# Attention scores: one DMA queue in place of two, and the last columns of the last tiles stored in three uneven pieces

## The chip, the core and the metric

The kernel runs on one core of one Trainium2 chip. A core has TensorE (PE), VectorE (DVE), ScalarE (ACT), GpSimd (POOL), SyncE (SP) and 16 DMA engines, which move data between the chip's main memory (HBM) and the core's working memory (SBUF). A DMA is issued by an engine's instruction queue (here SP's or ACT's) and its rows are dealt out over DMA engines. The metric is the device time of one execution in microseconds. Before the change it is 205.29 us, the median of three runs (205.13 to 205.38).

## The reference

```python
def setup_inputs():
    batch, heads, seq, dim = 8, 8, 512, 64
    # q, k: float32 of shape (8, 8, 512, 64)

def reference(q, k):
    scale = 1.0 / np.sqrt(q.shape[-1])
    return (np.einsum('bhqd,bhkd->bhqk', q, k) * scale).astype(np.float32)
```

For each of 64 pairs of batch and head, q times k transposed, scaled by 1/8. It reads 16.78 MB and writes 67.11 MB.

## The kernel before, in words

With B=8, H=8, S=512, D=64 the kernel's constants are P=128, G=4, M=32, R=16, RO=8, HP=2, U=64, JJ=2. It goes over the 8 batches.

- **Loads** (`load`, lines 53 to 58). For each batch one DMA for k (line 56) and one for q (line 57), each 1 MB: 128 partitions, in each two rows of 4 KB (heads 0 to 3 and 4 to 7). ACT's queue issues them. The raw tiles have four buffers, so four batches are loaded ahead (`AHEAD = 4`, lines 60 to 64); the load of batch b+4 stands in the code after the first two stores of batch b (lines 131 and 132).
- **Cast** (line 87): float32 to bfloat16, by DVE and ACT for the first batch, by POOL for all others.
- **Transposes**: PE transposes k (line 95) and q (line 103) into PSUM; DVE copies out kT (line 97), ACT qT (line 105).
- **Scores** (line 119): for each batch two groups `g0` (0 and 2) of two heads in each half `x`. A matmul gives 64 rows of 512 scores; eight of them fill two PSUM tiles.
- **Scaling** (`evacuate`, lines 68 to 75): ACT (line 71) and DVE (line 73) in turn multiply a PSUM tile by the scale and write it into an output tile.
- **Stores** (line 128): an output tile is 128 partitions of 8 x 512 float32, 16 KB per partition, 2 MB in all, contiguous in each partition and in HBM. There are two per group and four per batch, 32 in all, each stored by one DMA on SP's queue. The output tiles have six buffers: a buffer is written again when its store has landed.

The tile framework orders the instructions of each engine by its own planner, which may move an instruction ahead of its place in the code (the loads of the fifth batch go out before the first store). It also puts in the semaphores: DMA completions use eight of them in rotation, and the next DMA on a semaphore is issued only when the earlier one has landed.

Of the kernel before, what the change touches and what calls it, by code (L numbers as in the profile page):

```python
# [1 line left out]

# [5 lines left out]


@with_exitstack  # L10
def kernel(
    ctx: ExitStack,
    tc: tile.TileContext,
    q: bass.AP,
    k: bass.AP,
    out: bass.AP,
):

    nc = tc.nc
    B, H, S, D = q.shape
    scale = 1.0 / (D ** 0.5)
    P = 128
    G = H // 2
    M = P // G
    R = S // M
    RO = 8  # L30
    HP = RO * P // S
    U = P // HP
    JJ = R // RO

    f32 = mybir.dt.float32
    bf16 = mybir.dt.bfloat16

    q_r = q.rearrange("b (x g) (m j) d -> b (g m) x (j d)", x=2, j=R)
    k_r = k.rearrange("b (x g) (m j) d -> b (g m) x (j d)", x=2, j=R)
    out_r = out.rearrange("b (x n h) (u i) k -> b x n (h u) i k", x=2, h=HP, i=RO)  # L40

    consts = ctx.enter_context(tc.tile_pool(name="consts", bufs=1))
    raw_pool = ctx.enter_context(tc.tile_pool(name="raw", bufs=4))
    bf_pool = ctx.enter_context(tc.tile_pool(name="bf", bufs=2))
    t_pool = ctx.enter_context(tc.tile_pool(name="t", bufs=2))
    out_pool = ctx.enter_context(tc.tile_pool(name="out", bufs=6))
    tpsum_pool = ctx.enter_context(tc.tile_pool(name="tpsum", bufs=2, space=bass.MemoryType.PSUM))
    psum_pool = ctx.enter_context(tc.tile_pool(name="psum", bufs=3, space=bass.MemoryType.PSUM))

    AHEAD = 4  # L50
    raws = {}

    def load(b):
        kf = raw_pool.tile([P, 2, R * D], f32, name="kf")
        qf = raw_pool.tile([P, 2, R * D], f32, name="qf")
        nc.scalar.dma_start(out=kf, in_=k_r[b])  # L56
        nc.scalar.dma_start(out=qf, in_=q_r[b])  # L57
        raws[b] = (qf, kf)

    load(0)  # L60
    identity = consts.tile([P, P], dtype=bf16)
    make_identity(nc, identity)
    for b in range(1, AHEAD):
        load(b)

    n_evac = 0

    def evacuate(dst, src):
        nonlocal n_evac
        if n_evac % 2 == 0:  # L70
            nc.scalar.mul(out=dst, in_=src, mul=scale)  # L71
        else:
            nc.vector.tensor_scalar(out=dst, in0=src, scalar1=scale, scalar2=None,  # L73
                                    op0=mybir.AluOpType.mult)
        n_evac += 1

    for b in range(B):
        qf, kf = raws.pop(b)
        kb = bf_pool.tile([P, R, 2, D], bf16, name="kb")
        qb = bf_pool.tile([P, R, 2, D], bf16, name="qb")  # L80
        for slab, dst in ((kf, kb), (qf, qb)):
            for x in range(2):
                if b > 0:
                    copy = nc.gpsimd.tensor_copy
                else:
                    copy = (nc.vector.tensor_copy, nc.scalar.copy)[x]
                copy(out=dst[:, :, x, :], in_=slab[:, x].rearrange("p (j d) -> p j d", j=R))  # L87


        kT = t_pool.tile([P, P, R], bf16, name="kT")  # L90
        qT = t_pool.tile([P, RO, P, JJ], bf16, name="qT")
        for j0 in range(0, R, 8):
            tp = tpsum_pool.tile([P, 8, P], bf16, name="tp")
            for j in range(8):
                nc.tensor.transpose(out=tp[:, j, :], identity=identity,  # L95
                                    in_=kb[:, j0 + j].rearrange("p x d -> p (x d)"))
            nc.vector.tensor_copy(out=kT[:, :, j0:j0 + 8], in_=tp.rearrange("d j p -> d p j"))  # L97
        IW = 8 // JJ
        for i0 in range(0, RO, IW):
            tp = tpsum_pool.tile([P, IW, JJ, P], bf16, name="tp")  # L100
            for i in range(IW):
                for jj in range(JJ):
                    nc.tensor.transpose(out=tp[:, i, jj, :], identity=identity,  # L103
                                        in_=qb[:, RO * jj + i0 + i].rearrange("p x d -> p (x d)"))
            nc.scalar.copy(out=qT[:, i0:i0 + IW], in_=tp.rearrange("d i jj p -> d i p jj"))  # L105

        kTh = kT.rearrange("d (g m) j -> d g (m j)", g=G)
        qTh = qT.rearrange("d i (g m) jj -> d i g (m jj)", g=G)
        for g0 in range(0, G, 2):
            os = [out_pool.tile([P, 2 // HP, RO, S], f32, name="o") for _ in range(2)]  # L110
            for n in range(2 // HP):
                for i in range(0, RO, 2):
                    pss = [psum_pool.tile([P, 2, S], f32, name="ps") for _ in range(2)]
                    for w in range(2):
                        for h in range(HP):
                            g = g0 + n * HP + h
                            for x in range(2):
                                rows = slice(x * D, (x + 1) * D)
                                nc.tensor.matmul(out=pss[x][h * U:(h + 1) * U, w, :],  # L119
                                                 lhsT=qTh[rows, i + w, g, :],  # L120
                                                 rhs=kTh[rows, g, :],
                                                 start=True, stop=True,
                                                 tile_position=(x * D, h * U))
                    for x in range(2):
                        evacuate(os[x][:, n, i:i + 2, :], pss[x])
            for x in range(2):
                n0 = g0 // HP
                nc.sync.dma_start(  # L128
                    out=out_r[b, x, n0:n0 + 2 // HP].rearrange("n p i k -> p n (i k)"),
                    in_=os[x].rearrange("p n i k -> p n (i k)"))  # L130
            if g0 == 0 and b + AHEAD < B:
                load(b + AHEAD)


# [1 line left out]
_INS = ['q', 'k']  # L136
_OUTS = [((8, 8, 512, 512), 'float32')]


# [23 lines left out]
```

## Time and profile before

| | |
|---|---|
| median of 3 runs | 205.29 us |
| the profiled execution's own time | 205.29 us |
| its span, first to last instruction | 203.2 us |
| PE, DVE, ACT, POOL busy | 64%, 47%, 40%, 14% of the span |
| packets on the stores' queue and the loads' queue | 4608 and 4352 |
| mean DMA rate over the span | 413 GB/s |
| last store issued | 178.23 us |

The page gives, after the busy times, the span in 40 equal slices (5.08 us each): a digit is the busy share in tenths, and the row "DMA" is the mean over the core's 16 DMA engines. The queue lines give packets, megabytes and the share of the 16 engines' span that their packets took. A line of waits reads: engine and line, "<-" what it waited for, then us in total, how often, and the longest. The chain of waits follows the work that ended last back through what released it; its lines are start, duration and what it was. The view by stretches gives, for each, its length, the busy time and instruction count of PE, PE's weight loads, DVE, ACT and POOL, then PE's granted clock, the mean busy share of the DMA engines and GB/s; a transfer is counted where its packets start.

### The profile page before, as it was taken

The page shows a single profiled execution, that of the slowest core. Times are in us where ns is not written, and L with a number is a line of the kernel's source. Part 1 is how long each engine was busy: PE and PEld are TensorE (multiplying, and loading weights), DVE is VectorE, ACT ScalarE, POOL GpSimd, SP SyncE. Part 2 cuts the span into 40 slices and gives each one's busy share as a digit, 9 for nine tenths or more (in the row PEclk, how much of TensorE's full clock was granted, in tenths as well). Part 3 has the DMA queues.
Part 4 walks back from the last instruction along what each step waited for, and adds up shares of the span by engine and source line. Part 5 has one row for each costly group of instructions (what it writes and reads, how often), then busy time and mean ns, then how long its engine had stood idle before and what let it go on. Part 6 is the DMA issues. An engine that isn't in the chain of part 4 may idle for free.

```text
span 203.2 us, 1910 instructions
## 1 busy us (share of the span) xinstructions
PE 129.5 (64%) x768; PEld 46.5 (23%) x768; DVE 95.2 (47%) x82; ACT 81.9 (40%) x83; POOL 29.0 (14%) x34
## 2 busy tenths in 40 slices
PE   0187759997855099785997799779777777600000
PEld 0164314331520024210352135214211111000000
DVE  0247867567540291535853676276717180800000
ACT  0546753754852027242644273527551525200000
POOL 1077740303034003300030000000000000000000
PEclk9999985555785555555555555555555555555555
DMA  6999999999999999999999999999999999999991
GB/s 212 421 408 410 408 429 436 430 419 443 404 421 449 409 443 410 439 426 445 422 429 435 419 430 439 422 429 439 419 435 432 426 439 422 429 442 422 429 439 71
DMA packets 8968, 84.00 MB, mean 413 GB/s; under 512 B 768, under 2 KB 768, under 8 KB 4864
## 3 DMA queue, kind: packets, MB, share of 16 engines
q1 hardware_dynamic: 4608, 67.11, 77.3%
q10 hardware_dynamic: 4352, 16.78, 20.7%
q8 instruction: 6, 0.10, 0.2%
q14 instruction: 2, 0.02, 0.0%
HBM read 16.78 MB, written 67.11 MB: 413 GB/s over the span
## 4 chain that ended last, share of the span: by engine, by line
DMA 51%; DVE 17%; PE 14%; ACT 2%; POOL 1%; issue 1%; ACTq 1%; SPq 0%; DVEq 0%
DMA out_dram<-o 36%; DVE o L73 13%; DMA qf<-in_q_dram 11%; PE ps L119 10%; DVE kT L97 5%; DMA kf<-in_k_dram 4%; PE tp L95 2%; PE tp L103 2%; ACT o L71 2%; POOL kb L87 1%; ACT qT L105 1%; ACTq L56 0%; ACTq L57 0%; SPq L128 0%; DVEq L73 0%
## 5 line engine op out<-in xcount | busy, mean ns | idle before, releaser
L119 PE MATMUL ps<-kT,qT 64*64 64x512 bf16 x512 | 101.8, 584 | 35.2 <-DVE o L73 17.1
L73 DVE TENSOR_SCALAR o<-ps 128x1024 f32<-128x1024 f32 x64 | 75.7, 1220 | 70.1 <-DMA out_dram<-o 52.5
L71 ACT ACTIVATE o<-ps 128x1024 f32<-128x1024 f32 x64 | 63.9, 1022 | 84.5 <-PE ps L119 75.2
L119 PEld LDWEIGHTS <-qT 64*64 64x64 bf16 x512 | 24.0, 131 | 94.8 <-issue 91.7
L87 POOL CAST qb<-qf 128x1024 bf16<-128x1024 f32 x14 | 14.2, 1040 | 50.7 <-PE tp L103 33.5
L97 DVE COPY kT<-tp 128x1024 bf16<-128x1024 bf16 x16 | 18.8, 1217 | 5.3 <-PE tp L95 5.3
L95 PE MATMUL tp<-identity,kb 128*128 128x128 bf16 x128 | 14.8, 277 | 9.6 <-ACT kb L87 9.6
L103 PE MATMUL tp<-identity,qb 128*128 128x128 bf16 x128 | 16.4, 297 | 2.5 <-DVE kT L97 1.9
L105 ACT COPY qT<-tp 128x1024 bf16<-128x1024 bf16 x16 | 16.1, 1013 | 4.2 <-PE tp L103 4.2
L87 POOL CAST kb<-kf 128x1024 bf16<-128x1024 f32 x14 | 14.2, 1040 | 24.7 <-DMA kf<-in_k_dram 20.1
L95 PEld LDWEIGHTS <-kb 128*128 128x128 bf16 x128 | 10.4, 124 | 22.0 <-issue 11.5
L103 PEld LDWEIGHTS <-qb 128*128 128x128 bf16 x128 | 12.3, 136 | 12.5 <-issue 11.6
L87 ACT ACT_TABLE_LOAD x1 | 1.3, 1283 | 7.2 <-issue 7.2
L87 DVE CAST kb<-kf 128x1024 bf16<-128x1024 f32 x1 | 0.7, 694 | 5.6 <-DMA kf<-in_k_dram 5.6
L87 DVE CAST qb<-qf 128x1024 bf16<-128x1024 f32 x1 | 0.7, 694 | 1.9 <-DMA qf<-in_q_dram 1.9
L87 ACT CAST kb<-kf 128x1024 bf16<-128x1024 f32 x1 | 1.0, 1045 | 0.0
L87 ACT CAST qb<-qf 128x1024 bf16<-128x1024 f32 x1 | 1.0, 1039 | 0.0
masks.py:199 POOL TENSOR_SCALAR_AFFINE_SELECT identity<-identity 128x128 bf16<-128x128 bf16 x1 | 0.3, 292 | 0.1
masks.py:197 POOL MEMSET identity<- 128x128 bf16 x1 | 0.2, 205 | 0.3 <-POOLq L147 0.3
L147 POOL MEMSET const-float32-0.0<- 128x1 f32 x1 | 0.1, 98 | 0.2 <-issue 0.2
L147 POOL MEMSET const-bfloat16-1.0<- 128x1 bf16 x1 | 0.1, 101 | 0.0
L147 POOL MEMSET const-uint8-127<- 128x1 uint8 x1 | 0.1, 101 | 0.0
(1 smaller groups left out, 0.1 us busy)
## 6 DMA issues: line engine op xcount, KB each, us to landing
out_dram<-o SPq DMA_DIRECT2D x32, 2048.0 KB, 21.5
kf<-in_k_dram ACTq DMA_DIRECT2D x8, 1024.0 KB, 15.8
qf<-in_q_dram ACTq DMA_DIRECT2D x8, 1024.0 KB, 19.9
```

What stands on the lines that cost most here:

```text
L71: nc.scalar.mul(out=dst, in_=src, mul=scale)
L73: nc.vector.tensor_scalar(out=dst, in0=src, scalar1=scale, scalar2=None, op0=mybir.AluOpType.mult)
L87: copy(out=dst[:, :, x, :], in_=slab[:, x].rearrange("p (j d) -> p j d", j=R))
L95: nc.tensor.transpose(out=tp[:, j, :], identity=identity, in_=kb[:, j0 + j].rearrange("p x d -> p (x d)"))
L97: nc.vector.tensor_copy(out=kT[:, :, j0:j0 + 8], in_=tp.rearrange("d j p -> d p j"))
L103: nc.tensor.transpose(out=tp[:, i, jj, :], identity=identity, in_=qb[:, RO * jj + i0 + i].rearrange("p x d -> p (x d)"))
L105: nc.scalar.copy(out=qT[:, i0:i0 + IW], in_=tp.rearrange("d i jj p -> d i p jj"))
L119: nc.tensor.matmul(out=pss[x][h * U:(h + 1) * U, w, :], lhsT=qTh[rows, i + w, g, :], rhs=kTh[rows, g, :], start=True, stop=True, tile_posi ...
L147: nc = _bacc.Bacc("TRN2", target_bir_lowering=False, num_devices=1)
```

## The change

All loads are issued from SP's queue in place of ACT's, so that loads and stores share one queue. For the last two batches (8 output tiles, `b` of 6 and 7) a store is cut: the first 3584 columns of each partition (14 KB) are stored by one DMA, and the last 512 (2 KB) by three, over the partitions 0 to 111, 112 to 111+cut, and 112+cut to 127. `cut` goes from 15 to 8 over the eight tiles. So these tiles have four DMAs each, and there are 24 more in all.

```diff
     AHEAD = 4
+    CUTS = (15, 14, 13, 12, 11, 10, 9, 8)
     raws = {}
 
     def load(b):
         kf = raw_pool.tile([P, 2, R * D], f32, name="kf")
         qf = raw_pool.tile([P, 2, R * D], f32, name="qf")
-        nc.scalar.dma_start(out=kf, in_=k_r[b])
-        nc.scalar.dma_start(out=qf, in_=q_r[b])
+        nc.sync.dma_start(out=kf, in_=k_r[b])
+        nc.sync.dma_start(out=qf, in_=q_r[b])
         raws[b] = (qf, kf)
...
             for x in range(2):
                 n0 = g0 // HP
-                nc.sync.dma_start(
-                    out=out_r[b, x, n0:n0 + 2 // HP].rearrange("n p i k -> p n (i k)"),
-                    in_=os[x].rearrange("p n i k -> p n (i k)"))
+                dst = out_r[b, x, n0:n0 + 2 // HP].rearrange("n p i k -> p n (i k)")
+                src = os[x].rearrange("p n i k -> p n (i k)")
+                if b < B - 2:
+                    nc.sync.dma_start(out=dst, in_=src)
+                    continue
+
+                e = RO * S - 512
+                nc.sync.dma_start(out=dst[:, :, :e], in_=src[:, :, :e])
+                cut = CUTS[(b - B + 2) * 4 + g0 + x]
+                for p0, p1 in ((0, 112), (112, 112 + cut), (112 + cut, P)):
+                    if p1 > p0:
+                        nc.sync.dma_start(out=dst[p0:p1, :, e:], in_=src[p0:p1, :, e:])
             if g0 == 0 and b + AHEAD < B:
                 load(b + AHEAD)
```

## The prediction

> **What bounds the kernel now.** I read the time slices and the queues first, then the waits, then the end of the span in short stretches. The slices say that the 16 DMA engines are busy from the second slice to the last but one.
>
> ```profile
> DMA  6999999999999999999999999999999999999991
> GB/s 212 421 408 410 408 429 436 430 419 443 404 421 449 409 443 410 439 426 445 422 429 435 419 430 439 422 429 439 419 435 432 426 439 422 429 442 422 429 439 71
> ...
> q1 hardware_dynamic: 4608, 67.11, 77.3%
> q10 hardware_dynamic: 4352, 16.78, 20.7%
> ```
>
> The queue lines give packets, MB and the share of the 16 engines' span. 77.3% and 20.7% make 98%: queue 1 (the stores, issued from SP) and queue 10 (the loads, issued from ACT) fill the engines together. Nothing else can be the bound; the waits confirm it:
>
> ```profile
> ACT o L71 <- PE ps L119: 75.2, 42, 8.8
> DVE o L73 <- DMA out_dram<-o: 52.5, 11, 12.0
> ...
> PE tp L95 <- ACT kb L87: 9.6, 1, 9.6
> ...
> ACT L87 <- issue: 7.2, 1, 7.2
> ```
>
> DVE waits 52.5 us for output buffers that are still being stored, so arithmetic has slack. The DMA queue's own waits show what SyncE's issue queue (SP) does:
>
> ```profile
> SPq L128 <- ACT o L71: 109.2, 14, 12.4
> SPq L128 <- DMA qf<-in_q_dram: 29.4, 3, 19.2
> ```
>
> SP mostly waits for results. In three cases it waits for a load that its store does not need; the chain has one, where a load lands and the store goes out at once: the transfers share completion semaphores in rotation.
>
> ```profile
> 46.70 21.68 DMA qf<-in_q_dram
> 68.38 0.02 issue
> 68.40 0.02 SPq L128
> 68.42 0.03 issue
> 68.45 25.15 DMA out_dram<-o
> ```
>
> The stretches give, after the busy times, the granted clock, the DMA share and GB/s:
>
> ```profile
> 194.00:198.00 4.00, 0.00 (x0) 0.00 (x0) 0.00 (x0) 0.00 (x0) 0.00 (x0) 0.50 1.00 430
> 198.00:199.00 1.00, 0.00 (x0) 0.00 (x0) 0.00 (x0) 0.00 (x0) 0.00 (x0) 0.50 0.69 295
> 199.00:200.00 1.00, 0.00 (x0) 0.00 (x0) 0.00 (x0) 0.00 (x0) 0.00 (x0) 0.50 0.27 115
> 200.00:201.00 1.00, 0.00 (x0) 0.00 (x0) 0.00 (x0) 0.00 (x0) 0.00 (x0) 0.50 0.08 33
> 201.00:202.00 1.00, 0.00 (x0) 0.00 (x0) 0.00 (x0) 0.00 (x0) 0.00 (x0) 0.50 0.04 16
> ```
>
> A rate of 430 GB/s is 27 per engine. From 198 on engines run out of work one by one, and from 200 to 202 the rate is that of about one engine: a single late engine sets the end, nearly 2 us behind the next. The trace does not number the engines. That is the unknown of this case.
>
> **The change, part by part.** The sum is against the profiled execution: span 203.2 us and 2.09 us around it make 205.29, which is also the median of the three runs.
>
> Prices of a row. 77.3% of 16 engines for 203.2 us is 2513 us; over 4096 store rows of 16 KB, 0.6136 us each. 20.7% is 673 us; over 4096 load rows of 4 KB, 0.1643 us. A straight line through both is 0.0374 us per KB, so a row of 2 KB costs 0.0894 and one of 14 KB 0.5387. (Semaphore packets, 768 in all, are inside these.)
>
> *The cut.* In the last two batches, 8 tiles, each of 128 rows of 16 KB becomes one of 14 KB and one of 2 KB. I read the change at its word: 112 short rows are dealt 7 to an engine, the other 16 one to an engine from the lowest number up. Per tile the highest engine then has 7 short rows in place of 8, and over the 8 tiles 56 in place of 64; the lowest gets the second DMA's row as well as the third's, 9 per tile, 72. [...]
>
> Highest engine before: 64 x 0.6136 = 39.27 us. After, with the line: 64 x 0.5387 + 56 x 0.0894 = 39.49, so +0.22: the price of splitting 64 rows (0.0145 each, 0.93) is more than the relief (8 x 0.0894 = 0.72). No transfer of 2 KB rows is in the trace, so bounds. Below: a price by bytes alone (0.0767 and 0.5369) gives 38.66, so -0.61. Above: a short row costs as much as a 4 KB load row, 64 x 0.5387 + 56 x 0.1643 = 43.68, so +4.41. I take 0.100 per short row, a little over the line: of the two sizes seen, the smaller is the dearer per KB (0.041 against 0.038), and 2 KB lies outside both. 64 x 0.5387 + 56 x 0.100 = 40.08: **+0.81**. The completions of two more DMAs per tile that reach the highest or next engines I cost at nothing; the line already holds one per 8 rows.
>
> [...]
>
> *Loads from ACT to SP.* Sixteen issues leave ACT (374 to 2376 ns each) and join 32 stores on SP, which become 56: 24 more of 332 to 1150 ns.
>
> ```profile
> L128 SPq DMA_DIRECT2D out_dram<-o x32: 332/332/1150, 23.1 to 178.2; - x32
> ```
>
> Four issues per tile are 1.3 to 4.6 us, against 4.9 us in which a tile of 2.1 MB drains at 429 GB/s: covered, narrowly at the worst. On ACT the first activation waited 7.2 us for issue, and the first transposes 9.6 us for it; ACT could start its cast when the first tile lands (5.6 us), some 3 us sooner. That is worth nothing while the DMA engines are full. On SP a load waits behind stores and a store behind a load whose raw buffer is not free; both are covered by the backlog (a store lands 21.5 us after issue).
>
> What changes for the engines is mixing: two queues served in turn become one in order.
>
> ```profile
> 5.00:20.00 15.00, 8.24 (x80) 5.87 (x80) 7.23 (x7) 8.15 (x8) 7.55 (x8) 1.00 1.03 413
> 25.00:75.00 50.00, 34.43 (x222) 12.96 (x219) 27.81 (x25) 22.73 (x23) 10.79 (x11) 0.61 1.01 426
> 90.00:160.00 70.00, 57.68 (x304) 18.52 (x304) 39.96 (x34) 33.13 (x34) 2.02 (x2) 0.50 1.01 429
> ```
>
> Loads alone ran at 413, mixed at 426, stores alone at 429. The first five slices moved 9.4 MB, so 7.3 MB of loads fell in the mixed 50 us beside 14.0 MB of stores. Apart they take 7.3/413 + 14.0/429 = 17.7 + 32.6 = 50.3 us: **+0.3** at most, 0 at least if in-order transfers mix at their seams. I take 0.3, as every load then runs beside its like.
>
> *Completions.* With four transfers per tile in eight rotating semaphores, two tiles can be outstanding, where it was up to six buffers. When a tile's first part has landed the next tile, 4.9 us, is still queued. A 1 MB load alone took 4.8 us from issue to landing at best, of which 1.05/413 = 2.5 are data, so about 2.3 us start-up: covered, cost 0; uncovered only where an engine leads the late one by over 2.6 us, and leaders do not set the end.
>
> Sum: 203.2 + 0.81 + 0.3 = 204.3; with 2.09 around it, 206.4 us.
>
> **Rivals.**
> *Relief wins (faster).* The late engine is the highest, short rows cost their bytes and mixing costs nothing: -0.61, 204.7. It decides only if splitting a row costs under about 0.0035 us (56 x 0.0035 less the 0.61 is -0.41) and 0 for mixing. For it: one engine does end late. Against: the line says 0.0145.
> *A wash.* Highest engine, price on the line or under it, mixing 0 to 0.3: 205.0 to 205.7; this also holds if the late engine gains what the split costs.
> *The wrong engine.* If the late engine is one of the lowest, it gets 72 short rows: 64 x 0.5387 + 72 x 0.100 = 41.68, +2.41, with mixing 208.0 (207.2 on the line). The trace cannot exclude it, since it has no numbers; for it speaks nothing else.
> *Short rows collide.* Engines slow each other on short rows: up to +4.41 and 0.3, 210.0.
> *A hole at the start.* If SP places the fifth batch's loads behind the first store, the first 8.4 MB are done at about 22.8 us, the store went out at 23.10 and 2.3 us of start-up follow: up to 2.6 us idle; nothing if ACT's earlier start brings the store forward. On ACT the fifth load went out at 12.8, well ahead of its place in the code, so I expect the same on SP.
>
> **How the numbers follow.** A difference under about 0.2%, 0.41 us, can't be told from none. Chances: the forecast (slower by 0.4 to 2.3, 205.7 to 207.6) 0.42; wrong engine 0.11; collisions or a hole 0.14; a wash 0.17; relief wins 0.16. So faster 0.16, same 0.17, slower 0.67. The range leaves a tenth on either side: from 204.8 (just above the lower bound) to 209.6 (just under the upper).
>
> **What would show it.** Right: the DMA row still full; the share in the last stretches falling as before, with the last engine later by about 1 us; under 8 KB packets up by 1024; the stretch from 160 on below 429 GB/s; loads and stores in one queue line. The queue's share should grow by 0.5 to 1% of the engines' time: 1024 rows at 0.0145 to 0.025 are 15 to 26 us of engine time. Wrong: if the end falls steeply from full to empty and the rate after 160 stays at 430, relief won; if the rate after 160 falls to 390 or less, collisions; if the second slices show a dip, the hole.

## The result and the profile after

The changed kernel takes 210.13 us (median of four runs, 209.91 to 210.23), the kernel before 205.25 beside it: a ratio of 1.0236, 95% interval 1.0219 to 1.0254. It is slower, by 4.9 us. The profiled execution has a span of 208.1 us. All ratios are of runs in the chip's usual, fast state; one run of those below, the fourth of `rows32` (229.74 us), was in a slower one.

First the slices and queue lines of the changed kernel, the same parts of the page as shown of before.

```profile
DMA  5999999999999999999999999999999999989993
GB/s 216 420 410 410 440 419 400 435 438 422 423 425 443 416 435 412 434 427 431 435 400 435 438 422 438 422 431 438 419 439 427 422 412 381 396 337 361 362 377 103
...
q1 hardware_dynamic: 10240, 83.89, 97.5%
q8 instruction: 6, 0.10, 0.2%
q14 instruction: 3, 0.02, 0.0%
```

All loads and stores now go through queue 1, in 10240 packets. The engines stay full to the last slices, but in the last seven full slices the rate is 337 to 412 GB/s in place of some 430. Busy engines that move less: the packets themselves have become slower. 97.5% of 16 engines for 208.1 us is 3246 us of engine time; before it was 98.0% of 203.2, 3186. The 60 us more are 3.8 us for each engine.

The stretches place it. The columns are as before; the last two are the share of the DMA engines and GB/s.

```profile
5.00:20.00 15.00, 10.96 (x98) 6.87 (x100) 9.68 (x10) 8.70 (x9) 7.42 (x8) 1.00 1.03 413
25.00:75.00 50.00, 37.26 (x248) 14.66 (x245) 27.10 (x24) 24.99 (x26) 10.12 (x10) 0.68 1.01 426
90.00:160.00 70.00, 52.25 (x273) 16.66 (x273) 33.98 (x30) 30.73 (x31) 5.88 (x6) 0.55 1.01 429
...
170.00:180.00 10.00, 5.24 (x21) 0.85 (x19) 4.71 (x4) 3.72 (x4) 0.00 (x0) 0.50 1.00 389
180.00:190.00 10.00, 0.00 (x0) 0.00 (x0) 0.00 (x0) 0.00 (x0) 0.00 (x0) 0.50 0.97 370
190.00:200.00 10.00, 0.00 (x0) 0.00 (x0) 0.00 (x0) 0.00 (x0) 0.00 (x0) 0.50 0.94 348
```

Up to 160 us the three rates are those of before to the digit: 413, 426, 429. The loss begins with the cut stores, which flow from about 160 us on. The kernel before, from 170 to 195 us (its last rows end at 202):

```profile
170.00:195.00 25.00, 5.11 (x20) 0.84 (x19) 4.71 (x4) 2.98 (x4) 0.00 (x0) 0.50 1.01 433
```

The trace's packets tell the same: of the 1024 rows of 14 KB the median takes 535 ns but the mean 567 and the longest 1227; of the 1024 rows of 2 KB the median takes 84 ns, the mean 104. (567 - 535 + 104 - 84) x 64 rows is 3.3 us per engine, most of it in the long rows.

The issues are the second thing to see:

```profile
L140 SPq DMA_DIRECT2D out_dram<-o x24: 242/1204/1982, 148.0 to 201.0; - x24
```

SP needs 1.2 us on the median of these issues, where it needed 0.33 before, with one store per tile. With 0.8 us for the store of 14 KB rows, four per tile come to 4.4 us, not far from the 4.9 in which a tile of 2.1 MB drains at 429 GB/s. So two explanations were open: engines that get in each other's way, and an issue queue that can't keep up.

### The profile page after: what moved, and what is told of

Read it like the earlier page. It is cut to its first block, busy times and chain, and to the rows that moved or that the text cites. A ratio compares the mean times of both kernels' runs of the same rounds, so it can differ in the third digit from the quotient of the medians.

```text
span 208.1 us, 1939 instructions
## 1 busy us (share of the span) xinstructions
PE 129.5 (62%) x768; PEld 45.2 (22%) x768; DVE 94.5 (45%) x82; ACT 82.9 (40%) x83; POOL 29.0 (14%) x34
## 2 busy tenths in 40 slices
DMA packets 10249, 84.01 MB, mean 404 GB/s; under 512 B 1024, under 2 KB 1024, under 8 KB 6144
## 3 DMA queue, kind: packets, MB, share of 16 engines
q1 hardware_dynamic: 10240, 83.89, 97.5%
## 4 chain that ended last, share of the span: by engine, by line
DMA 65%; DVE 12%; PE 5%; ACT 4%; issue 1%; SPq 0%; DVEq 0%
DMA out_dram<-o 61%; DVE o L74 10%; PE ps L120 3%; DMA qf<-in_q_dram 3%; ACT o L72 2%; DVE kT L98 2%; ACT qT L106 1%; PE tp L96 1%; PE tp L104 0%; DVE qb L88 0%; SPq L57 0%; SPq L132 0%; DVEq L74 0%
## 5 line engine op out<-in xcount | busy, mean ns | idle before, releaser
L120 PEld LDWEIGHTS <-qT 64*64 64x64 bf16 x512 | 22.5, 124 | 110.7 <-issue 107.8
L96 PE MATMUL tp<-identity,kb 128*128 128x128 bf16 x128 | 13.4, 270 | 7.7 <-ACT kb L88 6.8
L104 PE MATMUL tp<-identity,qb 128*128 128x128 bf16 x128 | 15.1, 286 | 2.2 <-DVE kT L98 1.5
L104 PEld LDWEIGHTS <-qb 128*128 128x128 bf16 x128 | 11.7, 131 | 9.6 <-issue 8.6
L96 PEld LDWEIGHTS <-kb 128*128 128x128 bf16 x128 | 11.2, 125 | 11.5 <-ACT kb L88 6.8
```

Source lines behind the costliest of these rows:

```text
L96: nc.tensor.transpose(out=tp[:, j, :], identity=identity, in_=kb[:, j0 + j].rearrange("p x d -> p (x d)"))
L120: nc.tensor.matmul(out=pss[x][h * U:(h + 1) * U, w, :], lhsT=qTh[rows, i + w, g, :], rhs=kTh[rows, g, :], start=True, stop=True, tile_posi ...
```

## The experiments

The theories: *queue* (one queue in place of two costs), *split* (short rows cost in themselves), *issue* (four issues per tile are too slow, with two tiles outstanding), *collision* (a DMA that doesn't deal the partitions to the engines as a 128-partition DMA does makes engines slow each other), and the uneven shares. Which engine takes which row isn't in the trace: that a DMA of 112 or 16 rows is dealt otherwise than one of 128 is a premise of the collision theory. In the changed kernel's trace each DMA of 112 rows has 16 completions, and each of n rows, up to 15, has n, beside one update 0.4 to 1.9 us after the issue began; that the 112 rows go seven to an engine is the author's reading of the change. Each ratio is against runs of the kernel before on the same chip (medians of 205.25 to 205.42 us). The experiments ran on four chips, so a difference between two of them can be off by 0.1 to 0.2 us.

### One queue alone: `loads_sp`

```diff
-        nc.scalar.dma_start(out=kf, in_=k_r[b])
-        nc.scalar.dma_start(out=qf, in_=q_r[b])
+        nc.sync.dma_start(out=kf, in_=k_r[b])
+        nc.sync.dma_start(out=qf, in_=q_r[b])
```

> The kernel before with the loads issued from SP and nothing else changed. If the one queue costs (queue theory), this takes most of the 4.9 us: 208 to 210. If the cost lies in the cut stores (short rows, collisions between engines or SP's issue time), it is 205.1 to 205.6: up to 150 us the changed kernel had landed as many transfers as the one before, within 0.1 us.

Measured: 205.92 us, ratio 1.0032 (1.0021 to 1.0044): 0.64 us slower, so not most of the loss, but more than either side had said. The first engine completes the last store at 198.86 us after the span's start (198.76 before), the last one 4.31 us after it (3.65 before). The late engine alone makes the loss, and it falls back in one step: 3.35 us behind at the store that lands from 155, 4.03 at the next. At 162.3 us, within that, the trace has a fetch of 8 KB on queue 14, which it did not have before:

```profile
q14 instruction: 3, 0.02, 0.0%
```

In the kernel before the line reads

```profile
q14 instruction: 2, 0.02, 0.0%
```

SP had some 80 recorded instructions at the fetch; in the kernel before it gets to 76, and a fetch follows after the end. So the reading is: SP's sixteen more issues bring its instruction fetch into the run, and it fell to the late engine. The runs below support it. In six with loads on SP (the changed kernel, `split2`, `even3`, `rows32`, `cols4`, `stride4`) such a fetch comes at 149 to 157 us, and the last engine's distance grows by 0.5 to 0.7 us at the store in which it falls; in `aligned4` by 0.35. In `cut_act`, where it comes at 193.6, the distance doesn't grow; perhaps it fell to another engine.

### The cut alone: `cut_act`

```diff
 after.py, loads back on ACT
-        nc.sync.dma_start(out=kf, in_=k_r[b])
-        nc.sync.dma_start(out=qf, in_=q_r[b])
+        nc.scalar.dma_start(out=kf, in_=k_r[b])
+        nc.scalar.dma_start(out=qf, in_=q_r[b])
```

> The change's cut stores alone, loads left on ACT. Queue theory: 205.3 to 206.5. Cut theories: 209.5 to 210.5, the whole loss. If part of the loss comes from SP having loads to issue as well, something between, 207 to 209; but the last load is issued at 84 us and the loss begins after 150, so I expect the whole loss.

Measured: 209.94 us, 1.0226 (1.0211 to 1.0241). Nearly the whole loss is the cut's.

### Short rows on the usual partitions: `split2`

```diff
-                for p0, p1 in ((0, 112), (112, 112 + cut), (112 + cut, P)):
-                    if p1 > p0:
-                        nc.sync.dma_start(out=dst[p0:p1, :, e:], in_=src[p0:p1, :, e:])
+                nc.sync.dma_start(out=dst[:, :, e:], in_=src[:, :, e:])
```

> Loads on SP; the last eight tiles stored by two DMAs over all 128 partitions, 14 KB and 2 KB of each row. Split theory (a short row costs in itself): the packets seen in the changed kernel, 567 + 104 ns a row against 612, would give 64 x 0.059 = +3.8, so 209. Collision theory: with every engine on its usual partitions a short row costs its undisturbed 84 ns less 4 of overlap, 64 x 0.004 = +0.3, so 205.3 to 206. Issue theory: two issues per tile fit in 4.9 us, 205.3 to 206.

Measured: 206.31 us, 1.0048 (1.0031 to 1.0065), which is 0.39 above `loads_sp`. The packets are back at 535.6 and 84.0 ns on the mean, and hardly one is disturbed: of the 1024 long rows 13 take over 545 ns, of the short ones none over 91. Splitting a row costs 0.39/64 = 0.006 us; the split theory (209) falls.

### As many DMAs on the usual partitions: `aligned4` and `cols4`

```diff
 aligned4
+                for c0, c1 in ((e, e + 170), (e + 170, e + 341), (e + 341, e + 512)):
+                    nc.sync.dma_start(out=dst[:, :, c0:c1], in_=src[:, :, c0:c1])
 cols4, in place of the 14 KB store too
+                for c0 in range(0, RO * S, 1024):
+                    nc.sync.dma_start(out=dst[:, :, c0:c0 + 1024], in_=src[:, :, c0:c0 + 1024])
```

> Loads on SP; the last eight tiles stored by four DMAs each, as in the change, but all over 128 partitions: 14 KB, then 680, 684 and 684 bytes of each row. Issue theory (four issues per tile of up to 2 us on SP, and only two tiles outstanding): 208.5 to 210.5, and issues of more than 1 us each. Collision theory: every engine reads its usual partitions, so only the row prices, 3 x 64 short rows at some 10 ns of fixed cost: 206 to 207.5, with packets of 14 KB at 535 ns.

Measured: 208.24 us, 1.0142 (1.0127 to 1.0157). It lies between the two expectations and decides nothing: its packets of 680 and 684 bytes (34 ns each) raise the price of a row, and the 14 KB packets are at 543 ns on the mean; not all of its 2.3 us over `loads_sp` is accounted for. Hence the next one, with rows that are not so short.

> Loads on SP; each of the last eight tiles stored by four DMAs over all 128 partitions, 4 KB of each row: the same number of issues and bytes per DMA as with 32 full rows, every engine on its usual partitions. Collision theory: only the price of packets, about 64 x 4 x 0.003 us and 24 completions, 206 to 207. Issue theory: 208 to 210, with SP never waiting between issues.

Measured: 207.14 us, 1.0088 (1.0073 to 1.0103), 1.2 over `loads_sp` where up to 1.1 was expected from packets and 2 to 4 from issue. SP issues every 1.3 us here too, but the engines lack nothing (share 1.02 in the stretch below). So four issues per tile are not what costs 4 us.

### Even shares, other partitions: `even3`

```diff
-                cut = CUTS[(b - B + 2) * 4 + g0 + x]
-                for p0, p1 in ((0, 112), (112, 112 + cut), (112 + cut, P)):
+                for p0, p1 in ((0, 112), (112, P)):
```

> Loads on SP; the last eight tiles stored as 14 KB of all rows, then the short rows of partitions 0 to 111 and of 112 to 127 in two DMAs: every engine gets eight short rows as before the change, but not those of its usual partitions, and SP has three issues per tile. Collision theory: packets slow as in the change (14 KB well over 535 ns on the mean, 2 KB over 84), 207.5 to 209.5. Issue theory: three issues of up to 1.3 us fit in 4.9, so as with two, 206.3 to 206.6. Theory that the loss comes from the uneven shares: as with two, 206.3.

Measured: 210.43 us, 1.0249 (1.0234 to 1.0264): the whole loss with three issues per tile and, if the 112 rows go in sevens, with eight short rows for every engine. Beside a third issue per tile, only the cut of the short rows at partition 112 differs from `split2`, and it costs 4.1 us (4.0 with each run against the kernel before on its own chip). Issues aren't it: with four of them `cols4` loses 1.2 us in all. Which of the two pieces, 112 rows or 16, does the harm was not tried. Mean packets: 559 and 117 ns. By the same reading of the deal the uneven shares are not the cause either; the change itself is 0.2 to 0.3 us faster than this, about the width of the intervals.

### Which partitions are read together: `rows32` and `stride4`

Each of the last eight tiles stored by four DMAs of 32 full rows of 16 KB; in one the rows are neighbours, in the other every fourth. The lines stand in place of all stores of the cut.

```diff
 rows32
+                for p0 in range(0, P, 32):
+                    nc.sync.dma_start(out=dst[p0:p0 + 32], in_=src[p0:p0 + 32])
 stride4
+                for r in range(4):
+                    nc.sync.dma_start(out=dst[r::4], in_=src[r::4])
```

> Loads on SP; each of the last eight tiles stored by four DMAs of 32 partitions and full rows of 16 KB: no short row, equal shares, four issues per tile. [...] Issue theory: the time of four issues, 208 to 210. [...]

> As with four DMAs of 32 neighbouring partitions (221.8 us), but each DMA takes every fourth partition, r, r+4, ..., r+124, so that it spans all of SBUF. Rows, bytes, shares and issues are the same. Collision theory: the loss depends on which partitions are read together, so most of the 16.5 us over the kernel before goes: 206 to 213. If the loss came from DMAs of 32 rows, from two rows per engine or from SP's issues, it stays at 220 to 223.

Measured: 221.80 us with neighbours (three runs of 221.62 to 221.90), 1.0801 (1.078 to 1.0823); 206.77 us with every fourth, 1.0067 (1.0053 to 1.008). Same rows per DMA, bytes, packets (9344), issues and queue; only the partitions differ, and they are worth 15 us. From 166 us on a packet of 16 KB takes 852 ns on the mean in the one and 612 in the other. The same stretch, 170 to 200 us, first of `rows32`, then of `stride4`, `cols4`, `even3` and `split2`:

```profile
170.00:200.00 30.00, 5.62 (x25) 0.84 (x19) 4.71 (x4) 3.98 (x4) 0.00 (x0) 0.50 0.99 328
```

```profile
170.00:200.00 30.00, 5.33 (x21) 0.84 (x19) 4.71 (x4) 3.81 (x4) 0.00 (x0) 0.50 0.99 420
```

```profile
170.00:200.00 30.00, 5.48 (x22) 0.84 (x19) 4.71 (x4) 3.97 (x4) 0.00 (x0) 0.50 1.02 416
```

```profile
170.00:200.00 30.00, 5.36 (x22) 0.84 (x19) 4.71 (x4) 3.85 (x4) 0.00 (x0) 0.50 1.00 382
```

```profile
170.00:200.00 30.00, 5.33 (x21) 0.84 (x19) 4.71 (x4) 3.82 (x4) 0.00 (x0) 0.50 1.00 422
```

The engines are equally busy in all five (0.99 to 1.02); the rate is 416 to 422 where columns or stepped partitions are stored, 382 with an eighth of the bytes misplaced (`even3`), 328 where 32 neighbours are read together. With neighbours the time is 11.8 us over the 210 of the issue theory's upper end; with every fourth partition it lies in the 206 to 213 of the collision theory. What slows the packets of neighbours was not shown: the trace gives a packet's time, not what it waits for. Nor is it settled on which side they are slowed: each partition's row has a fixed place in HBM, so whoever changes the partitions that are read together changes the HBM rows that are written together as well (512 KB in one piece in `rows32`, every fourth 16 KB in `stride4`). No run here separates the two sides.

### Which engine is late: `marker`

```diff
 before.py, the last tile alone
+                nc.sync.dma_start(out=dst[:, :, :e], in_=src[:, :, :e])
+                for p0, p1 in ((0, 112), (112, 117), (117, 121), (121, P)):
+                    nc.sync.dma_start(out=dst[p0:p1, :, e:], in_=src[p0:p1, :, e:])
```

> The kernel before with the last store alone cut: 14 KB of all rows, then short rows by DMAs of 112, 5, 4 and 7 partitions. It numbers the late engine of the kernel before. If it is engine 4, as the small DMAs of the change suggest, one completion of the DMA of 5 rows comes some 2 to 4 us after its others, and none of the DMA of 4 rows does. If it is the highest (as forecast), neither has a late one, nor the DMA of 7. The time stays within 0.5 us of 205.3.

Measured: 206.16 us in one run, 0.8 above before and so a little over what was expected. Half of it, 0.4, stands before the cut: at the store ahead of it the late engine is at 197.92 us, in the kernel before at 197.56. A DMA of n such rows shows n completions in the trace, read here as one by each engine that takes part. The five of the second lie at 198.87, 198.91, 199.32, 199.54 and **202.95** us; the four of the third at 199.04 to 199.72; the seven of the last end with 201.32 and **203.14**. So the late engine takes part in a DMA of five rows but not in one of four. The sets look nested: in the changed kernel the completions of a DMA of two to four rows lie within 0.6 us of each other, while of five rows one is late, of six two, of seven three. Counted from 0 in the order in which small DMAs take engines, the late one is number 4, and so it is called here; that this is also its number in the hardware was not shown. In the changed kernel it is the same: its DMA of 5 rows has a completion at 190.08 where its others end at 186.65, and the one of 4 rows has none. At the end, though, it is no longer alone: of the DMA of 7 rows in the last tile but one, four engines complete at 199.33 to 199.57 us and three at 201.28 to 201.47. If the 112 rows go in sevens, engine 4 was given 7 + 1 short rows per tile in that kernel, and a ninth in the last four: 68 in place of 64, more and not less.

### The fetch once more: `half_sp`

```diff
-        nc.scalar.dma_start(out=kf, in_=k_r[b])
+        nc.sync.dma_start(out=kf, in_=k_r[b])
```

> Only k's loads go to SP, q's stay on ACT. With all loads on SP the profile shows an instruction fetch of 8 KB at 162 us, when SP has had some 80 instructions, and the late engine falls 0.7 us further behind at that time; before, SP reached 80 only at the end. Fetch theory: the fetch comes later, at 175 to 205; if it still falls on the late engine before its last rows, 205.9 again, else 205.3, and a step of the lateness stands at the fetch or not at all. Queue theory (one queue in order costs by the loads in it): half of 0.64, 205.6, with no step.

Measured: 206.57 us, 1.0056 (1.0043 to 1.007), worse than with all loads on SP, which neither theory said. The fetch comes at 187.6, when SP has had 79 recorded instructions, and the late engine steps from 3.95 to 4.55 us behind at that store: the fetch theory's step. The rest is another matter: the first engine ends at 199.33, 0.57 later than before, and the first slice moved 188 GB/s in place of 212, 0.12 MB or 0.3 us of data. Why k and q on two queues start slower is left open.

### Relief where it is needed: `relief_sp` and `relief_act`

```diff
 before.py, the last tile alone; the four small ones from SP or from ACT
+                for p in (slice(0, P, 2), slice(1, P, 4), slice(3, P, 8)):
+                    nc.sync.dma_start(out=dst[p], in_=src[p])
+                for p0 in range(7, P, 32):
+                    nc.scalar.dma_start(out=dst[p0:p0 + 25:8], in_=src[p0:p0 + 25:8])
```

> The kernel before with the last tile alone stored so that engine 4 gets less: full rows by DMAs of every second (64), every fourth (32) and every eighth partition (16), seven rows to each engine, and the last 16 rows by four DMAs of 4 rows, which go to engines 0 to 3. Engine 4 has one row of 16 KB fewer (-0.61), engines 0 to 3 three more (+1.8, from 2 to 3 us ahead). If spread partitions cost as little as in the stores with step 4 (0.1 us a tile), 204.6 to 205.1, faster than both kernels. If six more issues bring SP's instruction fetch into the run, it adds 0.6 to 0.7: 205.2 to 205.8. If several engines on one slice of SBUF still slow engine 4, 205.4 to 207.

> The same with the four DMAs of 4 rows issued from ACT, so that SP has only two more than before and they start beside the others rather than after them: 204.6 to 205.1 if the relief holds and no fetch falls in; 205.2 to 206 if ACT's own fetch or the collisions take it back.

Measured: 205.17 us from SP, 0.9989 (0.998 to 0.9998), and 204.92 us from ACT, 0.9981 (0.9972 to 0.999), against 205.36. The first lies a little above the 205.1 that was hoped for, the second within. A relief of the right engine with spread partitions gains 0.2 to 0.4 us and is faster than both kernels. In the profiled executions the late engine takes 4.3 us for the last tile in both, the time of seven rows in place of eight (7 x 0.611), so the relief itself came in full; but at the store ahead of it the engine was already 0.2 us later than in the kernel before (197.80 and 197.78 us, 197.56 before), for a cause that was not sought.

## Why the prediction was right or wrong

The forecast was slower, 206.4 in a range of 204.8 to 209.6; it is slower, but at 210.13, outside. By the runs the 4.85 us over 205.28 are made of: loads on SP +0.64, the split of rows +0.39 (`split2` less `loads_sp`), the cut of the short rows at partition 112 +4.12 (`even3` less `split2`), the uneven shares in place of even ones -0.30 (210.13 less 210.43). The last two compare different chips; with each run against its own kernel before they are +4.0 and -0.2.

- **What bounds the kernel**: right. The DMA engines were full and stayed nearly full; 3.8 of the 4.9 us are busy time of theirs.
- **The cost of the cut** is the term that failed: +0.81 in the sum, +4.66 measured with nothing else changed (`cut_act`). That the highest engine gets 56 short rows, on which the +0.81 rests, no run shows; the runs show how many completions a DMA has, and how long its packets take. The step that was wrong is that a row was priced by its size alone, whatever is stored beside it, and collisions stood in the sum with nothing. The price of a short row was not far off: 0.0894 on the line, 0.100 taken, 0.084 undisturbed in `split2`, where the split cost +0.39 for 64 rows. But with the short rows cut at partition 112 they take 0.104 us on the mean, and the 14 KB rows, which are stored as ever, 0.567 where 0.5387 was put in: 64 x (0.567 + 0.104 - 0.6136) is +3.7 for a mean engine. The upper bound (+4.41) was none for the same reason: it raised the short rows to a load's price and left the long ones untouched. That the two terms of the sum come to 1.11 and their parts without collisions to 1.03 (`split2` and `loads_sp`) is luck: one was too high, the other too low and for another cause.
- **Collisions** stood as a rival outside the sum, as no row of before showed any, and got 0.14 together with a hole. The result is 0.1 us above that rival's 210.0. The kind of loss was right, the agreement in size is luck: the rival put all of it into the short rows, at 164 ns, and these take 104; of the 52 ns that a pair of rows loses, 32 are in the long one. The sign that was named, a rate after 160 us that falls "to 390 or less", came: 389, 370, 348.
- **The late engine**: wrong. I took the highest, at whose relief the change aims by its description. It is the fifth that small DMAs take (engine 4), and by the reading of the deal it got 68 short rows in place of 64. The rival of the wrong engine was right that it isn't the one to be relieved, but that is not what cost the time: with eight short rows for every engine by that reading (`even3`) the loss is the same. Nor is the loss the late engine's own: the first engine to finish the last DMA of 112 rows does so at 204.46 us, where the first to finish the last store of before was done at 198.76; the last ones are at 206.91 and 202.41.
- **Loads on SP**: +0.3 for the end of mixing, measured +0.64, but none of it from mixing: the mixed stretch runs at 426 with one queue as with two. The queues did change as written: from 30 to 55 us the kernel before moves 541 load packets among 509 of stores, while the changed one has 475 of loads and 2 of stores from 32.5 to 37.5 us, and 392 of stores and none of loads from 40 to 55. The 0.64 came, by the reading above, from an instruction fetch, which I had not thought of. The hole at the start did not appear: the first store went out at 19.32 us in place of 23.10, and ACT's first cast no longer waits for its issues, as costed.
- **Issues and completions**: covered narrowly, as written; `cols4` shows that they do not bound. In the change itself the share of 0.94 to 0.97 leaves up to 0.9 us from 170 to 200 in which engines on the mean lack work; whether that touches the late engine was not tried. SP waited for loads in six cases before, not in three: beside the line for q that I read stands `SPq L128 <- DMA kf<-in_k_dram: 18.0, 3, 10.0`. Nothing in the sum rested on it.
- **The queue's share** was to grow by 15 to 26 us of engine time; it grew by 60. That line alone would not tell collisions from a dear split (0.059 us a row makes the same 60); the packets do, as more than half of them keep to 535 and 84 ns.

## What to carry to other kernels

In this kernel, which its DMA engines bound, the price of a DMA depended on its partitions too: an eighth of the bytes of eight tiles, stored by ranges of partitions beside whole tiles, cost 4 us, and slowed the other rows more than itself (32 ns against 20). A full engine row with falling GB/s was its mark (a share of 0.94 to 1.00 at 389 to 348 GB/s). Where a tile had to be cut, ranges of neighbours were dear and the rest was cheaper: over `loads_sp`, eight tiles in four ranges of 32 neighbours cost 15.9 us, in four sets of every fourth partition 0.85, in two pieces of columns 0.39 and in four of 4 KB a row 1.2, in four with pieces of 680 bytes 2.3. Where a tile must be cut, the cheaper of these are the first to try. Before work is taken off a late engine, find out which one it is: here DMAs of five and of four rows told it from their completions (one at 202.95 us among the five, none of the four after 199.72).

## What the hardware showed that I had not expected

- One DMA engine, number 4 in the order of small DMAs in the two kernels where that could be read (`marker` and the changed one), falls behind steadily: in the kernel before its last completion of a store comes 1.7 us after the first engine's at 97 us and 3.65 at 174, and then the distance stays. The matmuls end at about 177. In that time packets of 614 to 662 ns stand among the 611 of the others. The cause is not known.
- Instruction fetches take a DMA engine for about 1 us each: six of 16 KB (0.92 to 1.05 us) in the kernel before, at 24, 45, 77, 106, 133 and 168 us, and at the end six engines lie about 1.5 us behind the first; that the one makes the other was not tried. Where a fetch of 8 KB (0.31 us) fell to the late engine, the engine lost some 0.6 us, more than the fetch takes; why is not known. By that reading sixteen more issues on SP lengthened a kernel that is bound by transfers by 0.64 us (`loads_sp`).
